# Second MLP product of an encoder layer: a fifth inner product in doubled form, its side work moved

## The chip, the core and the metric

The kernel runs on one core of a Trainium2 chip. The metric is the device time of one launch in microseconds (us), from the first instruction to the last. TensorE (PE in the profile) multiplies, with its weight loads listed as PEld; VectorE (DVE), ScalarE (ACT) and GpSimd (POOL) work element by element; SyncE (SP) issues nearly all transfers, which sixteen DMA engines carry out.

## The reference

One encoder layer on a sequence of 2048 tokens with 1024 channels, in fp32. Only its last lines matter here:

```python
x = x + gt1 * (mixed @ w_o[l])
h = rmsnorm(x, g_norm2[l]) * (1.0 + sc2) + sh2
x = x + gt2 * (jnp.square(jax.nn.relu(h @ w1[l])) @ w2[l])
```

The first MLP product multiplies 2048x1024 by `w1` (1024x4096), the second 2048x4096 by `w2` (4096x1024). What stands ahead of them (modulation, input projection, two kinds of attention) is not touched.

## The kernel before

Everything is held transposed: channels on the 128 partitions, 512 tokens (`TB`) to a tile. A number in fp32 is split into a rounded high part and the rest (`split`): ScalarE copies the high part, VectorE subtracts it from the number to get the low part. A product is then three matmuls, high by high, high by low, low by high (`mm3`, line 206). The pair of parts of one 128x512 tile is called an operand here. It lies in one of the 8 buffers of the pool `opp` (line 1297).

**Seven products instead of eight.** Both MLP products are written as 2x2 block products by Strassen's method in Winograd's form. The seven inner products are numbered `OUTER` = 1, 5, 6, 3, 7, 2, 4; each is the product of a sum of blocks of the weights and a sum of blocks of the activations.

**The order of the work.** A list `steps` is run from front to back. Ahead of each step operands of later steps are prepared as long as no more than 8 tiles are held (line 1949). Other work is hung on a step's number by `at(n, job)`. PE and SP run in the order in which the program issues; a scheduler sets the order of VectorE and ScalarE when the program is built, and it is fixed from then on. The second half of the kernel is this list:

- 8 `Mixed` steps: rest of the output projection.
- For `mb` = 1: 112 `First` steps (16 column pairs `j` by seven inner products): the first MLP product for half of the tokens. A step is 12 matmuls. Its results are relu'd, squared, and kept as block sums in `scr_hid` in HBM.
- `plain(1, i)` for `i` in `PLAIN` (line 1284): inner product `i` of the second MLP product for `mb` = 1, 16 `Second` steps of 12 matmuls each (4 output tiles by 3).
- For `mb` = 0: 112 `First` steps again.
- `plain(0, 1)`, `outer(7)`, `plain(0, 6)`, `outer(2)`, `plain(0, 5)`, `outer(3)`, `outer(4)` (line 1891 on).

**The doubled form.** `outer(i)` (line 1791) does inner product `i` of both halves `mb` at once by a second level of the same method: again seven products `pr`, each of 8 `Outer` steps with 6 matmuls, so 56 steps and 336 matmuls, where the plain form takes 192 for each `mb`. It needs more besides. An `Outer` step takes one operand `opr` of the activations, and every second step one operand `ol` of the weights: 84 operands. `half` loads activation sums into `halves`, and `half_sum` makes three more sums of them, for `pr` = 6, 7 and 4 (4 subtractions on VectorE each, 128x1024). `outer_sums` (line 1677) makes the weight sums of the second level beforehand, during the `First` steps of `mb` = 0, and stores them in `scr_t`. When a product ends, its PSUM result is added straight into tiles of the residual by `weigh` (lines 1627 and 1761): one tile for `i` = 2, 3 and 4, two for `i` = 7, at six of the products and for two banks each, so 12 or 24 instructions. The plan for `half` and `half_sum` is written down by step numbers (lines 1894 to 1902), the gap between the four of one kind being two steps.

**Plain products** instead collect 1, 6 and 5 in a shared sum `Second.whole["s", n]` in SBUF, and `update` (line 1634) loads residual tiles, adds that sum by `weigh`, and stores them: after product 6 four tiles, after product 5 twelve, for each `mb`.

**The second normalization** of `mb` = 0 (`norm2`) leaves its row factors in `rows`, in the two buffers of pool `rp`. `right_blocks` (line 1372) then makes the right-hand blocks of the first MLP product out of the residual for each of 4 values `k`: load, multiply by the factors, shift, and a chain of splits and subtractions (15 on VectorE per `k`). For `mb` = 0 this runs beside `plain(1, ...)`, ten steps to a `k`, in six pieces.

## Time and profile before

| | |
|---|---|
| median of three runs | 2552.38 us (2550.7 to 2552.95) |
| the profiled execution | 2549.72 us, span 2548.0 us |
| busy in the span | PE 99%, PEld 83%, DVE 79%, ACT 59%, POOL 29% |
| granted TensorE clock | 1.00 in every slice |
| transfers | 698.92 MB, mean 274 GB/s |
| second half of the kernel, from 1315.47 us | `First` of `mb` = 1 from 1359.0, plain products from 1668.4, `First` of `mb` = 0 from 1798.9, `plain(0, 1)` from 2103.57, `outer(7)` from 2149.37, `plain(0, 6)` from 2226.37, `outer(2)` from 2270.24, `plain(0, 5)` from 2346.40, `outer(3)` from 2389.92, `outer(4)` from 2466.08 |

In a line of the trace the names of tiles tell the stage: `opw` and `h` belong to `First`, `oph` and `opv` to the plain products, `opr`, `ol` and `r` to the doubled ones (`r<-r,r` is a `half_sum`), `txo` and `cxo` to `weigh` in a doubled product, `txu` and `xu` to `update`. Nearly all lines stand under L42, since a helper records the operations. A matmul's duration in the trace (389 ns) contains the pipeline; what it costs is the time from one start to the next. The same holds for VectorE, whose instructions begin a little before the one ahead of them has ended.

### The profile page before, as it was taken

The numbers are of one execution on the slowest core, as the hardware profiler recorded it, in microseconds if no ns is written. First come the engines' busy times: TensorE is split into PE (matmuls) and PEld (weight loads), VectorE is DVE, ScalarE is ACT, GpSimd is POOL, SyncE is SP. The second block draws the span as 40 slices with busy tenths as digits, with TensorE's granted clock in tenths as the row PEclk, the third lists the DMA queues.
The fourth block names the chain that finished last, engine by engine and source line by source line (L and its number), as shares of the span: only waits on it lengthen the run. The fifth ranks groups of instructions, "written<-read, shape, count | busy, mean of one in ns | idle before, by whom it ended". The sixth has DMA issues, their size and how long they took to land.

```text
span 2548.0 us, 39355 instructions
## 1 busy us (share of the span) xinstructions
PE 2520.9 (99%) x12436; PEld 2104.0 (83%) x12436; DVE 2010.0 (79%) x3509; ACT 1498.6 (59%) x2871; POOL 747.0 (29%) x1128
## 2 busy tenths in 40 slices
PE   9999999999999999999999999999999999999999
PEld 7888888888888888887988888888888887888887
DVE  7656767887789878998858777668988766988897
ACT  6333425668866677666755555566555555656565
POOL 4330154776776667776620000000000000000000
PEclk9999999999999999999999999999999999999999
DMA  9879979779987788866787888787899889777772
GB/s 359 327 295 365 348 269 295 216 243 291 284 237 235 239 251 269 268 211 196 230 301 253 301 284 281 257 312 260 279 323 303 264 274 394 273 285 271 281 266 83
DMA packets 293200, 698.92 MB, mean 274 GB/s; under 512 B 31360, under 2 KB 83584, under 8 KB 281856
## 3 DMA queue, kind: packets, MB, share of 16 engines
q1 hardware_dynamic: 291696, 691.69, 79.7%
q10 hardware_dynamic: 1296, 4.72, 0.5%
q8 instruction: 98, 1.61, 0.3%
q14 instruction: 110, 0.90, 0.1%
HBM read 477.66 MB, written 218.63 MB: 273 GB/s over the span
## 4 chain that ended last, share of the span: by engine, by line
PE 83%; DVE 6%; DMA 3%; ACT 3%; issue 2%; POOL 1%; SPq 0%; DVEq 0%; ACTq 0%; POOLq 0%
PE ps L42 27%; PE ps_s L42 14%; PE pt L42 11%; PE acc L42 6%; PE wt L42 6%; PE pf L42 4%; PE z L42 4%; PE po L42 4%; PE pq L42 3%; DVE p L42 2%; PE cz L42 2%; DMA hw<-in_w_dram 1%; PE ct L42 1%; DVE opr L42 1%; ACT z L42 1%
## 5 line engine op out<-in xcount | busy, mean ns | idle before, releaser
L42 PE MATMUL ps<-h,opw 128*128 128x512 f32 x1512 | 358.6, 389 | 0.0
L42 ACT CAST wth<-wt 128x512 fp32r<-128x512 f32 (+3 forms) x544 | 257.3, 484 | 166.0 <-PE wt L42 156.9
L42 POOL TENSOR_TENSOR b<-p 128x512 f32<-128x512 f32 (+1 forms) x320 | 292.5, 914 | 168.0 <-DVE p L42 95.0
L42 DVE TENSOR_TENSOR wtl<-wt,wth 128x512 fp32r<-128x512 f32 (+3 forms) x544 | 291.2, 547 | 57.6 <-ACT wth L42 55.8
L42 PEld LDWEIGHTS ps<-h,opw 128*128 128x128 f32 x1512 | 283.7, 188 | 58.8
L42 PE MATMUL pt<-w,ht 128*128 128x512 f32 x1248 | 288.2, 391 | 0.0
L42 PE MATMUL ps_s<-h,opw 128*128 128x512 f32 x1152 | 277.3, 389 | 0.4 <-ACT ps_s L42 0.4
L42 PEld LDWEIGHTS pt<-w,ht 128*128 128x128 f32 x1248 | 232.9, 188 | 47.7
L42 DVE TENSOR_TENSOR_SCAN p<-z,p,zero 128x512 f32<-128x512 f32 x192 | 245.8, 1281 | 25.7 <-ACT z L42 18.1
L42 PE MATMUL ps<-oph,opv 128*128 128x512 f32 x1152 | 263.2, 390 | 1.2 <-ACT opv L42 1.1
L42 PEld LDWEIGHTS ps<-oph,opv 128*128 128x128 f32 x1152 | 216.0, 188 | 47.8 <-ACT opv L42 1.9
L42 PEld LDWEIGHTS ps_s<-h,opw 128*128 128x128 f32 x1152 | 215.9, 188 | 46.0 <-ACT ps_s L42 0.8
L42 PE MATMUL acc<-wth,v 128*128 128x512 f32 (+3 forms) x544 | 220.6, 410 | 0.0
L42 ACT CAST opr<-r 128x512 fp32r<-128x512 f32 x224 | 139.7, 625 | 105.5 <-PE ps L42 50.6
L42 ACT ACTIVATE z<-z 128x512 f32<-128x512 f32 (+1 forms) x320 | 166.4, 520 | 55.3 <-PE z L42 48.9
L42 PE MATMUL z<-k,q 128*128 128x512 f32 (+3 forms) x640 | 185.7, 372 | 7.7 <-DVE p L42 7.0
L42 PE MATMUL acc<-wtl,v 128*128 128x512 f32 (+3 forms) x544 | 185.5, 347 | 0.0
L42 PE MATMUL ps<-opr,ol 128*128 128x512 f32 x768 | 176.4, 389 | 0.1
L42 PE MATMUL wt<-ident,b 128*128 128x128 f32 x1088 | 171.4, 273 | 0.9 <-DVE p L42 0.6
L42 DVE TENSOR_TENSOR opr<-r,opr 128x512 fp32r<-128x512 f32 x224 | 151.3, 689 | 25.9 <-ACT opr L42 23.3
L42 PEld LDWEIGHTS wt<-ident,b 128*128 128x128 f32 x1088 | 136.4, 141 | 41.4 <-DVE wtl L42 1.9
L42 PEld LDWEIGHTS ps<-opr,ol 128*128 128x128 f32 x768 | 144.0, 188 | 30.5 <-DVE ol L42 0.4
(214 smaller groups left out, 4846.9 us busy)
## 6 DMA issues: line engine op xcount, KB each, us to landing
q<-scr_q SPq DMA_DIRECT2D x128, 256.0 KB, 5.5
w<-in_w_dram SPq DMA_DIRECT2D x64, 512.0 KB, 5.5
r<-scr_hid SPq DMA_DIRECT2D x64, 512.0 KB, 8.0
k<-scr_k SPq DMA_DIRECT2D x240, 128.0 KB, 4.5
v<-scr_v SPq DMA_DIRECT2D x120, 256.0 KB, 4.2
wa<-in_w_ada_dram SPq DMA_DIRECT2D x48, 512.0 KB, 6.2
ow<-scr_wo SPq DMA_DIRECT2D x24, 1024.0 KB, 6.2
hw<-scr_hid SPq DMA_DIRECT2D x48, 512.0 KB, 6.4
```

The lines of the kernel that those rows point to most:

```text
L42: return lambda *x, **y: self.tc.keep_in_program_order(f(*x, **y))
```

## The change

Inner product 5 of the second MLP product moves from the plain to the doubled form. `PLAIN` becomes 1 and 6, `DOUBLE` 7, 5, 2, 3, 4, and the order behind the `First` steps of `mb` = 0 becomes `plain(0, 1)`, `outer(7)`, `plain(0, 6)`, `outer(5)`, `outer(2)`, `outer(3)`, `outer(4)`. With it:

- `outer(5)` adds into two residual tiles per bank (24 instructions). Its activation blocks need one more subtraction (`half_sum` for `pr` = 5, four of 128x1024), which runs in `outer(7)`.
- The weight sums are made for 7, 5, 3 and 4 in the `First` steps of `mb` = 0, seven steps earlier than before; those of product 2 are made in the second half of the `First` steps of `mb` = 1, by the new `narrow_sums` (32 subtractions of 128x256 instead of 16 of 128x512 elements).
- The twelve `update` tiles that followed product 5 move. Those of `mb` = 1 go into the first half of the `First` steps of `mb` = 0, four steps apart, in the two buffers of pool `rp` that held the norms; those of `mb` = 0 go into `outer(2)` (eight) and `outer(3)` (four).
- `right_blocks` for `mb` = 0 runs in ten pieces (the new `chain`), six steps to a `k`, since there are 32 plain steps of `mb` = 1 now instead of 48.
- The step numbers of `half` and `half_sum` change.

In numbers of built instructions: 48 matmuls fewer, 72 transfers more, and on VectorE 20 operand parts, 16 half sums, 24 `weigh` and 32 narrow sums more and 8 `column_sum` into the shared sum fewer.

```diff
@@ -1281,8 +1281,8 @@
     NP = DFF // P // 2
     HK = KT // 2
-    PLAIN = (1, 6, 5)
-    DOUBLE = (7, 2, 3, 4)
+    PLAIN = (1, 6)
+    DOUBLE = (7, 5, 2, 3, 4)
     OUTER = (1, 5, 6, 3, 7, 2, 4)
     OUTER_NAME = {1: "11", 2: "12", 4: "22"}
     HOME = {1: 1, 2: 1, 5: 5, 3: 5, 6: 6, 7: 6, 4: 6}
@@ -1429,7 +1429,16 @@
                 low(6, "22")
                 low(4, "21")
-            return load, scale, mixed, rest, multiply, shift, begin
+            def chain():
+                yield low(1, "11"), low(3, "22"), less("11", "12", "11")
+                yield high(5, "11"), low(2, "21"), less("12", "22", "12")
+                yield high(7, "12"), low(5, "11"), less("22", "22", "11")
+                yield high(6, "22"), low(7, "12"), less("21", "21", "22")
+                yield high(4, "21"), low(6, "22")
+                yield low(4, "21"), None
+
+            steps_of = chain()
+            return load, scale, mixed, rest, multiply, shift, begin, lambda: next(steps_of)
         class Step:
@@ -1621,8 +1630,6 @@
                     act.copy(d["s", n], ps)
                 if i == 6:
                     column_sum(dve, d["s", n], ps, d["s", n], ALU.add)
-                if i == 5:
-                    column_sum(dve, d["s", n], ps, d["s", n], ALU.add)
         def weigh(x, a, n):
             dve.scalar_tensor_tensor(x, a, mod[:, 5 * KT + n : 5 * KT + n + 1], x, op0=ALU.mult, op1=ALU.add)
@@ -1653,25 +1660,9 @@
             f = len(steps)
             steps.extend(Second(mb, i, j) for j in range(NP))
-            spread = lambda *ns: [f + n for n in ns]
             if i == 6:
+                spread = lambda *ns: [f + n for n in ns]
                 update(mb, 0, 1, spread(0, 1, 2, 8), spread(4, 5, 6, 12))
-            if i == 5:
-                update(mb, 1, 1, spread(1, 2, 3, 9), spread(6, 7, 8, 13))
-                wide = []
-
-                def slot(nm):
-                    if not wide:
-                        t = raw_pair([P, HK, TB], F32, nm)
-                        wide.extend(t[:, n, :] for n in range(HK))
-                    return wide.pop(0)
-
-                if mb:
-                    update(mb, 0, 0, spread(11, 11, 11, 11), spread(16, 16, 17, 17), slot)
-                    update(mb, 1, 0, spread(13, 13, 14, 14), spread(18, 18, 19, 19), kept)
-                else:
-                    update(mb, 0, 0, spread(11, 12, 13, 14), spread(16, 17, 18, 19))
-                    update(mb, 1, 0, spread(15, 16, 17, 21), spread(20, 21, 22, 25), None, True)
             return f
         def outer_sums(i, m, step):
@@ -1681,7 +1672,7 @@
             def load():
                 t.append(raw_pair([P, 2, 2, TB], F32, f"wt{i}_{m}"))
                 for a in range(2):
-                    if i in (3, 7):
+                    if i in (3, 7, 5):
                         sp.dma_start(t[0][:, a], scr_s[i - 1 if i < 7 else 0, HP // 2 * a + m])
                         continue
                     r, s = {2: (0, 1), 4: (1, 1)}[i]
@@ -1695,6 +1686,27 @@
                 later.add(2, lambda: sp.dma_start(scr_t[i, pr][:, 2 * m : 2 * m + 2, :], v[dst]))
             at(step - 6, load)
+            todo = ((5, "22", "21", "22", ALU.add), (7, "21", "11", "21", ALU.subtract))
+            todo += ((6, "11", "22", "11", ALU.subtract), (3, "12", "12", "11", ALU.subtract))
+            for n, x in enumerate(todo):
+                at(step + n, lambda x=x: sums(*x))
+
+        def narrow_sums(i, k, step):
+
+            t = []
+            r, s = {2: (0, 1), 4: (1, 1)}[i]
+
+            def load():
+                for a in range(2):
+                    t.append(temp(f"wn{i}_{k}_{a}"))
+                    sp.dma_start(t[a], w2[2 * (HP * a + k) + s][:, r * TB : (r + 1) * TB])
+
+            def sums(pr, dst, a, b, op):
+                v = {nm: t[h][:, c * CN : (c + 1) * CN] for nm, h, c in (("11", 0, 0), ("12", 1, 0), ("21", 0, 1), ("22", 1, 1))}
+                column_sum(dve, v[dst], v[a], v[b], op)
+                later.add(2, lambda: sp.dma_start(scr_t[i, pr][:, k, :], v[dst]))
+
+            at(step - 4, load)
             todo = ((5, "22", "21", "22", ALU.add), (7, "21", "11", "21", ALU.subtract))
             todo += ((6, "11", "22", "11", ALU.subtract), (3, "12", "12", "11", ALU.subtract))
             for n, x in enumerate(todo):
@@ -1717,7 +1729,7 @@
                     sp.dma_start(t, scr_t[i, pr])
                     return
                 a, h = {1: (0, 0), 2: (1, 0), 4: (1, 1)}[pr]
-                if i in (3, 7):
+                if i in (3, 7, 5):
                     for m in range(HP // 2):
                         src = scr_s[i - 1 if i < 7 else 0, HP // 2 * a + m]
                         sp.dma_start(t[:, 2 * m : 2 * m + 2], src[:, :, h * CN : (h + 1) * CN])
@@ -1764,14 +1776,14 @@
                             later.add(2, lambda dst=dst, x=x: sp.dma_start(dst, x))
             def load_x(self, b):
-                home = kept if self.i == 7 and b in ("22", "11") else temp
+                home = kept if self.i in (5, 7) and b in ("22", "11") else temp
                 for n in range(2):
                     Outer.outs[b, n] = []
-                    for r, odd in {2: ((0, 1),), 3: ((0, 0),), 4: ((1, 1),), 7: ((1, 1), (1, 0))}[self.i]:
+                    for r, odd in {2: ((0, 1),), 3: ((0, 0),), 4: ((1, 1),), 7: ((1, 1), (1, 0)), 5: ((0, 0), (1, 0))}[self.i]:
                         mb, row = 2 - int(b[1]), HK * r + 2 * (int(b[0]) - 1) + n
                         x = home(f"xo{self.i}_{b}_{n}{odd}")
                         sp.dma_start(x, scr_x[2 * mb + odd, row])
-                        Outer.outs[b, n].append((x, mb, row, odd, self.i != 7 or (mb and not odd)))
+                        Outer.outs[b, n].append((x, mb, row, odd, self.i in (2, 3, 4) or (self.i == 5 and mb and r)))
         halves = {}
@@ -1783,6 +1795,9 @@
         def half_sum(i, pr, g):
+            if pr == 5:
+                column_sum(dve, halves[5, g], halves[5, g], halves[1, g], ALU.subtract)
+                return
             x, y = {6: (3, 5), 7: (6, 1), 4: (2, 6)}[pr]
             t = hop[g].tile([P, 2, TB], F32, tag=f"h{pr}_{g}", name=f"r{i}_{pr}_{g}")
             column_sum(dve, t, halves[x, g], halves[y, g], ALU.subtract)
@@ -1858,8 +1873,10 @@
                 f = steps[begin + 7 * j]
                 if mb:
                     second_sums(j, begin + 7 * j + 2)
+                    if j >= HP:
+                        narrow_sums(2, j - HP, begin + 71 + 5 * (j - HP))
                 else:
-                    outer_sums(DOUBLE[j // 4], j % 4, begin + 7 * j + 5)
+                    outer_sums((7, 5, 3, 4)[j // 4], j % 4, begin + 7 * j - 2)
                     if j < HP:
                         for i, n in ((3, 2), (2, 5), (7, 2), (4, 5)):
                             at(begin + 7 * j + n, lambda i=i, f=f: f.other(i))
@@ -1872,14 +1889,19 @@
                 norm2(1, begin + 18)
                 norm2(0, begin + 48)
                 for k in range(HK):
-                    begins = end + 1 + 10 * k
-                    pieces = right_blocks(0, k, temp)
-                    for n, m in ((0, 0), (4, 4), (5, 5), (6, 6), (7, 2), (9, 3)):
+                    begins = end + 6 * k
+                    pieces = right_blocks(0, k, kept if k % 2 else temp)
+                    for n, m in ((0, 0), (4, 4), (5, 5), (6, 6), (7, 7), (8, 7), (9, 7), (10, 7), (11, 7), (12, 7)):
                         at(begins + n, pieces[m])
                 for i in PLAIN:
                     plain(1, i)
                 for n in range(end, len(steps), 2):
                     at(n - 7 - max(0, end + 4 - n) // 2, steps[n].load)
+                rest = len(steps)
+                lent = lambda nm: rp.tile([P, TB], F32, tag="r", name=nm)
+                for n, (r, odd) in enumerate(((0, 0), (1, 1), (1, 0))):
+                    at_row = rest + 3 + 16 * n
+                    update(1, r, odd, range(at_row, at_row + 16, 4), range(at_row + 4, at_row + 20, 4), lent)
             else:
                 at(begin - 8, steps[begin].load)
                 at(begin - 6, steps[begin].fetch)
@@ -1889,17 +1911,25 @@
                 at(f + m - (leads.pop(0) if leads else 7), steps[f + m].load)
         f = plain(0, 1)
-        plain_loads(f, [9])
+        plain_loads(f, [9, 9, 9, 8, 8, 8])
         e = len(steps)
-        plan = {"load": {1: (f - 5, 1), 5: (f - 1, 1), 3: (f + 4, 2), 2: (f + 18, 2)}}
-        plan["sum"] = {6: (f + 9, 2), 7: (f + 13, 2), 4: (f + 44, 2)}
-        for i, p in ((7, 6), (2, 5), (3, None), (4, None)):
+        plan = {"load": {1: (f - 3, 1), 5: (f + 2, 2), 3: (f + 10, 2), 2: (f + 18, 2)}}
+        plan["sum"] = {6: (f + 16, 2), 7: (f + 21, 2), 4: (f + 44, 2)}
+        for i in DOUBLE:
             f = outer(i, plan)
             e = len(steps)
-            if p:
-                plain_loads(plain(0, p), [12, 11, 11, 11, 9, 8])
-            plan = {"load": {1: (f + 6, 2), 5: (f + 17, 2), 3: (f + 30, 2), 2: (f + 46, 2)}}
-            plan["sum"] = {6: (e + 1 if i == 7 else f + 38, 2), 7: (e + 4, 2), 4: (e + 8, 2)}
+            if i == 7:
+                plain_loads(plain(0, 6), [12, 11, 11, 11, 9, 8])
+            spread = lambda *ns: [f + n for n in ns]
+            if i == 2:
+                update(0, 0, 0, spread(18, 22, 26, 30), spread(24, 28, 32, 36))
+                update(0, 1, 1, spread(36, 40, 44, 48), spread(42, 46, 50, 54))
+            if i == 3:
+                update(0, 1, 0, spread(12, 16, 20, 24), spread(17, 21, 25, 29), None, True)
+            plan = {"load": {1: (f + 22, 2), 5: (f + 17, 2), 3: (f + 30, 2), 2: (f + 46, 2)}}
+            plan["sum"] = {6: ({7: e + 1, 5: e - 4}.get(i, f + 38), 2), 7: (e + (8 if i == 7 else 16), 2), 4: (e + (16 if i == 7 else 26), 2)}
+            if i == 7:
+                plan["sum"][5] = (f + 31, 2)
         blocks = [right_blocks(1, k, kept if k else temp) for k in range(HK)]
```

## Prediction, made before the changed kernel ran

> **What bounds the kernel now.** I read the busy times first, then the chain of work that ended last, then the busy times stage by stage, and then single instructions inside the doubled products.
>
> ```profile
> PE 2520.9 (99%) x12436; PEld 2104.0 (83%) x12436; DVE 2010.0 (79%) x3509; ACT 1498.6 (59%) x2871; POOL 747.0 (29%) x1128
> PE 83%; DVE 6%; DMA 3%; ACT 3%; issue 2%; POOL 1%; SPq 0%; DVEq 0%; ACTq 0%; POOLq 0%
> ```
>
> TensorE is busy 99% and carries 83% of the chain: the time is its number of matmuls times its pace, plus what it waits. The stages, in order: the first row is `First` of `mb` = 1, the next three the plain products 1, 6, 5 of `mb` = 1, then `First` of `mb` = 0, `plain(0, 1)`, `outer(7)`, `plain(0, 6)`, `outer(2)`, `plain(0, 5)`, `outer(3)`, `outer(4)`. The first number behind the window is its length, then busy times.
>
> ```profile
> 1359.00:1668.37 309.37, 309.00 (x1378) 255.66 (x1376) 224.28 (x358) 173.32 (x306) 3.62 (x10) 1.00 0.79 277
> 1668.37:1711.89 43.52, 43.52 (x194) 36.05 (x192) 32.21 (x53) 27.50 (x49) 0.00 (x0) 1.00 0.80 290
> 1711.89:1755.41 43.52, 43.52 (x194) 36.05 (x192) 36.28 (x60) 29.28 (x52) 0.00 (x0) 1.00 0.69 255
> 1755.41:1798.93 43.52, 43.52 (x194) 36.05 (x192) 40.60 (x67) 26.51 (x47) 0.00 (x0) 1.00 0.83 290
> 1798.93:2103.57 304.64, 304.64 (x1346) 252.34 (x1344) 233.12 (x370) 161.65 (x285) 0.00 (x0) 1.00 0.88 289
> 2103.57:2149.37 45.80, 44.66 (x193) 35.82 (x192) 26.82 (x40) 21.10 (x38) 0.00 (x0) 1.00 1.04 402
> 2149.37:2226.37 77.00, 76.90 (x338) 62.83 (x336) 74.86 (x115) 51.03 (x88) 0.00 (x0) 1.00 0.80 291
> 2226.37:2270.24 43.87, 43.83 (x193) 35.96 (x192) 39.71 (x55) 18.57 (x32) 0.00 (x0) 1.00 0.74 287
> 2270.24:2346.40 76.16, 76.16 (x337) 63.06 (x336) 66.19 (x102) 50.57 (x86) 0.00 (x0) 1.00 0.73 261
> 2346.40:2389.92 43.52, 43.52 (x193) 36.04 (x192) 34.16 (x49) 18.31 (x32) 0.00 (x0) 1.00 0.79 287
> 2389.92:2466.08 76.16, 76.16 (x337) 63.06 (x336) 70.55 (x110) 50.58 (x86) 0.00 (x0) 1.00 0.80 282
> 2466.08:2543.80 77.72, 77.37 (x337) 62.58 (x335) 66.71 (x100) 46.99 (x80) 0.00 (x0) 1.00 0.37 127
> ```
>
> A doubled product's 336 matmuls take 76.16 us (0.2267 us each, 1.36 us a step of six), a plain product's 192 take 43.52. VectorE's share in a doubled product is 86 to 97%, against 74% in the first plain one. So VectorE is the second bound there, and the change puts four such products in a row without the plain product that stood between 2 and 3. Here is where TensorE already loses time in them, and in `plain(0, 1)`:
>
> ```profile
> 2131.64 6.01 PE L42 MATMUL ps<-oph,opv 128*128 128x512 f32 x24 [0.71 <-ACT opv L42]
> 2182.01 11.04 PE L42 MATMUL ps<-opr,ol 128*128 128x512 f32 x48
> 2192.89 11.44 PE L42 MATMUL ps_s<-opr,ol 128*128 128x512 f32 x48
> 2204.17 11.48 PE L42 MATMUL ps<-opr,ol 128*128 128x512 f32 x48
> 2215.49 11.04 PE L42 MATMUL ps_s<-opr,ol 128*128 128x512 f32 x48
> ...
> 2487.86 6.30 PE L42 MATMUL ps_s<-opr,ol 128*128 128x512 f32 x25
> 2494.41 5.90 PE L42 MATMUL ps_s<-opr,ol 128*128 128x512 f32 x23 [0.25 <-DVE opr L42]
> 2500.14 11.04 PE L42 MATMUL ps<-opr,ol 128*128 128x512 f32 x48
> ```
>
> Eight steps should go by in 10.88 us. In `outer(7)` steps 32 to 40 took 11.28 (2192.89 to 2204.17) and steps 40 to 48 took 11.32: 0.84 lost. In `outer(4)` steps 16 to 24 took 12.28 (2487.86 to 2500.14): 1.40 lost. `plain(0, 1)` lost 45.80 - 43.52 = 2.28, on transfers (below).
>
> VectorE's prices are the times from one start to the next:
>
> ```profile
> 2185.35 0.69 DVE L42 TENSOR_TENSOR ol<-l,ol 128x512 fp32r<-128x512 f32 x1
> 2185.96 1.29 DVE L42 TENSOR_TENSOR opr<-r,opr 128x512 fp32r<-128x512 f32 x2
> 2187.16 0.69 DVE L42 TENSOR_TENSOR ol<-l,ol 128x512 fp32r<-128x512 f32 x1
> ...
> 2189.57 1.22 DVE L42 TENSOR_TENSOR r<-r,r 128x1024 f32<-128x1024 f32 x1
> 2190.70 1.29 DVE L42 TENSOR_TENSOR opr<-r,opr 128x512 fp32r<-128x512 f32 x2
> ...
> 2194.25 2.72 DVE L42 SCALAR_TENSOR_TENSOR txo<-ps,mod,txo 128x512 f32<-128x512 f32 x4
> 2196.88 0.69 DVE L42 TENSOR_TENSOR opr<-r,opr 128x512 fp32r<-128x512 f32 x1
> ```
>
> A low part of an operand costs 0.602 us (1.81 for three), a half sum 1.13, a `weigh` 0.657 (2.63 for four); an `update` I take like a `weigh`.
>
> **The change part by part.**
>
> *Matmuls.* Out go 2 x 192 = 384, in come 336: 48 x 0.2267 = 10.9 us less. TensorE is the bound, so all of it counts.
>
> *VectorE in the doubled products.* I count the instructions between the first operand part of one stage and that of the next, in the built order. Before: `outer(7)` 84 operand parts, 10 half sums, 20 weighs = 75.0 us; `outer(2)` 65.2; `outer(3)` 71.1; `outer(4)` 68.8. Against 76.16 all fit. After:
> - `outer(7)`: 84 parts (50.6), 16 half sums (18.1; its own twelve now all lie inside it, and the four for `pr` = 5 are new), 20 weighs (13.1): 81.8, which is 5.6 too many.
> - `plain(0, 6)`: 32.4 of 43.52, room for 11.
> - `outer(5)`: 71.8.
> - `outer(2)`: 84 parts, 16 half sums, 14 weighs, 7 updates: 82.5, which is 6.3 too many.
> - `outer(3)`: 75.3, and `outer(4)` 68.8 as before.
>
> A mean is not enough: VectorE works its list in the built order, and only as far ahead as eight operand tiles allow. So I keep an account of its lag. A step gives it 1.36 us, and 1.5 operand parts take 0.90, so it gains 0.46 a step until it is level; every sum sets it back 1.13, a pair of weighs 1.31, four 2.63. What lag does TensorE bear? Before, in `outer(7)`, sums at steps 28 to 34 and four weighs at 32 and 40 make a lag of 4.4, then 4.3, and 0.84 was lost; in `outer(4)`, eight sums at steps 4 to 14 and two weighs make 5.8, and 1.40 was lost. Both say that about 4 us are borne (3.5 to 4.4) and the rest is lost.
>
> After, `outer(7)`: eight sums at steps 0 to 11 and four weighs at 8 make 6.6, so 2.6 lost; level by 24; eight sums at 28 to 37 and four weighs at 24 and 32 make 8.4, so 4.4 lost; four weighs at 40 add 1.3. Sum 8.3. `outer(5)`: its weighs at the end meet the first sums of the next product at a lag of 5.0: 1.0. `outer(2)`: pairs of sums and updates from step 16 to 54 make 8.3, so 4.5 lost. `outer(3)`: sums at 16 to 44 make 7.4, so 3.4 lost. `outer(4)`: 0.5. Together 17.7 if 4 us are borne, 20 at 3.5, 14.4 at 4.5; the lower end is the overload of the means less 4 us carried over at each of the two places, 4. I take 16, near the account since it is gauged in the same stages. Less the 2.2 lost there before: 13.8 more.
>
> One page speaks harder against this change. The Trainium skill, "VectorE: DVE Perf Modes", section "The DRAIN you can't avoid", says that the next operation does not start until the pipe has emptied, so that whole durations would add up (0.69, 1.22 and 0.68): `outer(7)` would then need 91 us and `outer(2)` 92, the five products would lose some 45, and the time would be near 2588. The rows differ: starts lie 0.60 apart at a duration of 0.69, and `outer(3)` of before, which would need 80 by that rule, lost nothing. The measurement decides.
>
> *Weight sums and loads of `plain(0, 1)`.* It gets its data with less crowding: its half sums move into `outer(7)`, the weight sums end seven steps earlier. Of the 2.28 lost I let 2.0 go; bounds 0 and 2.28. ScalarE, whose busy time in the doubled stages is at most 51 of 76, stays cover.
>
> *Plain products of `mb` = 1.* The four chains of `right_blocks` now lie in 32 steps instead of 48. In the built order VectorE has 38.7 us of work in `plain(1, 1)` and 47.8 in `plain(1, 6)`, of 43.52 each: 4.3 too many in the second, before which there is room. Bounds 0 and 4.3; I take 1.5, since a plain step uses two tiles in 2.72 us, and lag is borne for longer.
>
> *Narrow sums.* In the second half of `First` of `mb` = 1 come 16 loads, 32 stores and 32 subtractions; VectorE's mean there is 72% (224.28 of 309.37), so it is cover. What can be late is one sum that waits for its load, with the reads of PSUM queued behind it. The nearest row of a `First` stage:
>
> ```profile
> DVE ts L42 <- DMA scr_hid<-to: 11.9, 7, 2.2
> ```
>
> The longest was 2.2: bounds 0 and two of those, 4.4; I take 1.5.
>
> *Updates and transfers in `First` of `mb` = 0.* Twelve `update` tiles with 24 transfers come into its first half, where the DMA engines are at their highest of any stage with full pace:
>
> ```profile
> 1875.00:1913.00 38.00, 38.00 (x170) 31.46 (x169) 31.39 (x51) 20.33 (x36) 0.00 (x0) 1.00 0.98 321
> 2126.00:2149.00 23.00, 21.86 (x93) 16.93 (x92) 13.89 (x20) 11.03 (x21) 0.00 (x0) 1.00 1.05 405
> ```
>
> The last number is GB/s, the one ahead of it the engines' busy share. 24 x 0.262 MB over 152 us are 41 GB/s more on 321; at the highest share that any row has (1.05, where TensorE lost time) this mix would carry 321 x 1.05 / 0.98 = 344. So up to 5% of 152 us, 8, could be late (a bound, since some of these transfers lay there before); 0 if it fits. The two buffers of `rp` make it worse: each is loaded again one step after its store, and behind that load SP's whole queue waits. I take 3.
>
> *Sum:* -10.9 + 13.8 - 2.0 + 1.5 + 1.5 + 3 = +6.9 us on the profiled 2549.72. That run stands 2.7 below the median of 2552.38; on the median I forecast 2559.3.
>
> **The rivals.**
>
> *Faster.* VectorE's lag costs TensorE little: the four operand tiles ahead bear 7 or 8 us rather than 4, so that only the overload of the means counts. Then 4 are lost in the doubled products instead of 16, and with nothing lost in the `First` stages the sum is -10.9 + 1.8 - 2.3 + 1 = -10, or 2542. For it: `outer(3)` of before, at 93% busy, lost nothing. Against it: both places where before lost time fit 4 us. It decides from a borne lag of about 6 us, where the sum crosses zero.
>
> *Transfers fall behind* in the first half of `First` of `mb` = 0: the 8 above, 4.4 in `First` of `mb` = 1, 3 in the plain products, the rest as forecast: -10.9 + 13.8 - 2 + 15.4 = +16, or 2569. For it: share 0.98 with 8% more to carry. Against it: most of that work waits there with a long lead.
>
> *The clock falls.* The granted clock is 1.00 in all rows, through a gap of 0.71 us too. A group of 48 matmuls at half the pace would cost another 10.9, and one in each of `outer(7)`, `outer(2)` and `outer(3)` would make 2592. The lost time comes in pieces no longer than a burst of weighs, so I give it little. The Trainium skill, "TensorE: Matmul & The Clock Gate", section "What's actually happening", has the clock fall to half after an idle window of some 3.4 us; no stretch of before is that idle, so no run here shows it.
>
> **How the numbers follow.** Forecast 0.62, faster rival 0.14, transfers 0.20, clock 0.04. A measurement here tells 0.2% (5.1 us) from no change, so slower begins at 2557.5. Of the forecast, whose own range is 2554 to 2567 (the borne lag from 5 down to 3.5), 0.44 lies above that and 0.18 within; of the faster rival 0.11 lies below 2547.3; of the transfers 0.20 and of the clock 0.04 above. So faster 0.11, same 0.21, slower 0.68. The range, with a tenth left out on each side: 2550 to 2572.
>
> **What would show it.** `outer(7)` about 84 us long and `outer(2)` about 81, with VectorE over 95% busy and TensorE waiting there for VectorE's `opr`; `outer(5)` near 77; `plain(0, 1)` near 43.7; `First` of `mb` = 0 at 305 to 308. I would be wrong if those two products stayed near 77, or if TensorE's waits named transfers instead.

## The result, and the profile after

The change makes the kernel 0.6% slower: 2566.96 us (median of four runs, 2565.59 to 2571.0) against 2551.98 us for the kernel before on the same chip (2550.7 to 2552.95). The ratio is 1.0062, with a 95% interval of 1.0044 to 1.0079: small, but clear of the noise. The forecast was 2559.3 with a range of 2550 to 2572. The profiled execution took 2567.03 us with a span of 2565.3, which is 17.3 more than the span of before.

The page of after, busy times and the chain of work that ended last:

```profile
PE 2523.2 (98%) x12388; PEld 2094.1 (82%) x12388; DVE 2054.8 (80%) x3593; ACT 1509.6 (59%) x2893; POOL 747.5 (29%) x1128
PE 71%; DVE 14%; DMA 7%; ACT 3%; issue 3%; POOL 1%; SPq 0%; DVEq 0%; ACTq 0%; POOLq 0%
```

TensorE has 48 instructions fewer, as announced. Its share of the chain fell from 83 to 71%; VectorE's rose from 6 to 14% and that of the transfers from 3 to 7%. Both are to be looked for in the stages. Busy times by stage in after: `First` of `mb` = 1, both plain products of `mb` = 1 together, `First` of `mb` = 0, `plain(0, 1)`, `outer(7)`, then behind `plain(0, 6)` `outer(5)`, `outer(2)`, `outer(3)`, `outer(4)`. The columns are those of the same view in the prediction.

```profile
1358.90:1668.55 309.65, 309.00 (x1377) 255.66 (x1376) 234.17 (x389) 172.86 (x306) 3.62 (x10) 1.00 0.85 299
1668.55:1757.33 88.78, 88.22 (x385) 71.94 (x384) 79.29 (x130) 64.27 (x113) 0.00 (x0) 1.00 0.77 285
1757.33:2074.83 317.50, 307.15 (x1345) 251.59 (x1344) 239.73 (x383) 161.96 (x288) 0.00 (x0) 1.00 0.88 298
2074.83:2118.35 43.52, 43.52 (x193) 36.05 (x192) 23.04 (x36) 21.18 (x38) 0.00 (x0) 1.00 0.89 348
2118.35:2201.87 83.52, 80.37 (x337) 62.22 (x336) 82.00 (x120) 50.87 (x88) 0.00 (x0) 1.00 0.75 282
...
2245.73:2321.89 76.16, 76.16 (x337) 63.06 (x336) 72.37 (x113) 50.46 (x86) 0.00 (x0) 1.00 0.74 270
2321.89:2403.71 81.82, 79.34 (x337) 62.26 (x336) 80.64 (x119) 50.41 (x86) 0.00 (x0) 1.00 0.78 268
2403.71:2483.82 80.11, 79.00 (x337) 62.31 (x336) 76.66 (x115) 50.00 (x86) 0.00 (x0) 1.00 0.90 307
2483.82:2560.90 77.08, 76.77 (x337) 62.72 (x335) 66.84 (x101) 46.93 (x80) 0.00 (x0) 1.00 0.39 132
```

Compared with the rows of before, stage by stage:

| stage | before | after | loss or gain |
|---|---|---|---|
| 48 matmuls fewer | | | -10.9 |
| the doubled products, over 76.16 each | 0.84 + 0 + 0 + 1.56 = 2.4 | 7.36 + 0 + 5.66 + 3.95 + 0.92 = 17.9 | +15.5 |
| `First` of `mb` = 0 | 304.64 | 317.50 | +12.9 |
| `plain(0, 1)` | 45.80 | 43.52 | -2.3 |
| plain products of `mb` = 1 | 43.52 each | 88.78 for two | +1.7 |
| `First` of `mb` = 1 | 309.37 | 309.65 | +0.3 |
| `plain(0, 6)`, and ahead of and behind these stages | | | +0.1 |
| sum | | | +17.3 |

So there are two large losses of nearly the same size: one in three doubled products, which was expected, and one in `First` of `mb` = 0, which was expected to be 3. The first of them in TensorE's timeline of after, from the start of `outer(7)` to its end:

```profile
2118.35 22.23 PE L42 MATMUL ps<-opr,ol 128*128 128x512 f32 x96
2140.43 12.06 PE L42 MATMUL ps_s<-opr,ol 128*128 128x512 f32 x48
2152.32 11.04 PE L42 MATMUL ps<-opr,ol 128*128 128x512 f32 x48
2163.20 5.83 PE L42 MATMUL ps_s<-opr,ol 128*128 128x512 f32 x25
2169.73 2.03 PE L42 MATMUL ps_s<-opr,ol 128*128 128x512 f32 x6 [0.70 <-DVE opr L42]
2172.07 3.77 PE L42 MATMUL ps_s<-opr,ol 128*128 128x512 f32 x12 [0.31 <-DVE opr L42]
2176.15 1.44 PE L42 MATMUL ps_s<-opr,ol 128*128 128x512 f32 x5 [0.31 <-DVE opr L42]
2177.42 6.80 PE L42 MATMUL ps<-opr,ol 128*128 128x512 f32 x25
2185.27 5.88 PE L42 MATMUL ps<-opr,ol 128*128 128x512 f32 x23 [1.04 <-DVE opr L42]
2190.99 11.04 PE L42 MATMUL ps_s<-opr,ol 128*128 128x512 f32 x48
```

From start to start, where eight steps should take 10.88: steps 0 to 16 took 22.08 (0.32 lost), 16 to 24 took 11.89 (1.01), 32 to 40 took 14.22 (3.34), 40 to 48 took 13.57 (2.69). TensorE waits for `opr`, which VectorE brings late. VectorE's timeline of after at that place:

```profile
2164.62 0.68 DVE L42 TENSOR_TENSOR opr<-r,opr 128x512 fp32r<-128x512 f32 x1
2165.22 1.21 DVE L42 TENSOR_TENSOR r<-r,r 128x1024 f32<-128x1024 f32 x1
2166.36 2.72 DVE L42 SCALAR_TENSOR_TENSOR txo<-ps,mod,txo 128x512 f32<-128x512 f32 x4
2169.00 0.68 DVE L42 TENSOR_TENSOR opr<-r,opr 128x512 fp32r<-128x512 f32 x1
```

It works without a gap. Between one `opr` (2164.62) and the next (2169.00) lie a half sum and four weighs, 4.38 us in which TensorE could have taken three steps.

The second loss: TensorE's waits in `First` of `mb` = 0 of after (us in total, times, longest). The same view of before lists no wait at all.

```profile
PE ps_s L42 <- DVE cp L42: 8.1, 6, 1.7
PE ps_s L42 <- ACT cp L42: 2.2, 2, 1.6
```

`cp` is the read of a PSUM bank that TensorE needs again; VectorE and ScalarE read it too late. What VectorE waited for in the first half of the stage (157 us), in after:

```profile
DVE ts L42 <- DMA scr_hid<-to: 23.5, 6, 5.2
```

In before the same row (in the prediction) had 11.9 in total and 2.2 at the longest. `ts` is a temporary tile that is free again when the store of the `to` that lay in it has landed. One of these waits in VectorE's timeline of after, and then the bank that came late in TensorE's:

```profile
1834.75 0.68 DVE L42 TENSOR_TENSOR wt<-wt 128x512 f32<-128x512 f32 x1
1840.65 0.69 DVE L42 TENSOR_TENSOR ts<-w 128x512 f32<-128x512 f32 x1 [5.22 <-DMA scr_hid<-to]
```

```profile
1849.01 3.03 PE L42 MATMUL ps_s<-h,opw 128*128 128x512 f32 x12 [1.57 <-ACT cp L42]
...
1856.34 3.06 PE L42 MATMUL ps_s<-h,opw 128*128 128x512 f32 x12 [1.58 <-DVE cp L42]
```

And what SP's queue waited for in that half, where all these stores are issued, in after:

```profile
SPq L42 <- DMA scr_x<-xu: 24.1, 10, 4.3
```

In before the row of the same name stands at 0.7:

```profile
SPq L42 <- DMA scr_x<-xu: 0.7, 2, 0.4
```

So ten times the queue stood until the store of an updated tile `xu` had landed, because the next thing in it was a load into that tile's buffer. Everything behind, the stores of `to` among it, was issued later. These views do not show that the one wait caused the other; that is the reading from which the experiments start.

### The profile page after: what moved, and what is told of

Read it like the earlier page. It is cut to its first block, busy times and chain, and to the rows that moved or that the text cites. A ratio compares the mean times of both kernels' runs of the same rounds, so it can differ in the third digit from the quotient of the medians.

```text
span 2565.3 us, 39482 instructions
## 1 busy us (share of the span) xinstructions
PE 2523.2 (98%) x12388; PEld 2094.1 (82%) x12388; DVE 2054.8 (80%) x3593; ACT 1509.6 (59%) x2893; POOL 747.5 (29%) x1128
## 4 chain that ended last, share of the span: by engine, by line
PE 71%; DVE 14%; DMA 7%; ACT 3%; issue 3%; POOL 1%; SPq 0%; DVEq 0%; ACTq 0%; POOLq 0%
PE ps L42 19%; PE pt L42 11%; PE ps_s L42 10%; PE acc L42 6%; PE wt L42 6%; PE pf L42 4%; PE z L42 4%; PE po L42 4%; DVE opr L42 3%; PE pq L42 3%; DVE r L42 2%; DVE p L42 2%; DMA scr_t<-wt 1%; PE cz L42 1%; DMA scr_hid<-to 1%
## 5 line engine op out<-in xcount | busy, mean ns | idle before, releaser
L42 ACT CAST opr<-r 128x512 fp32r<-128x512 f32 x280 | 174.2, 623 | 146.0 <-PE ps L42 69.7
L42 PE MATMUL ps<-opr,ol 128*128 128x512 f32 x960 | 223.6, 391 | 2.3 <-DVE opr L42 1.9
L42 PEld LDWEIGHTS ps<-opr,ol 128*128 128x128 f32 x960 | 179.2, 188 | 44.2 <-DVE opr L42 5.3
L42 DVE TENSOR_TENSOR opr<-r,opr 128x512 fp32r<-128x512 f32 x280 | 185.8, 686 | 18.3 <-ACT opr L42 17.0
L42 PE MATMUL ps_s<-opr,ol 128*128 128x512 f32 x720 | 172.9, 394 | 4.7 <-DVE opr L42 3.9
L42 PE MATMUL ps<-oph,opv 128*128 128x512 f32 x768 | 176.0, 390 | 0.6 <-DVE oph L42 0.2
L42 PEld LDWEIGHTS ps<-oph,opv 128*128 128x128 f32 x768 | 143.9, 188 | 32.2 <-DVE oph L42 1.2
```

Source lines behind the costliest of these rows:

```text
L42: return lambda *x, **y: self.tc.keep_in_program_order(f(*x, **y))
```

## The experiments

Each stands beside runs of the kernel before on the same chip. The theory had two parts. In the doubled products, VectorE's lag is what TensorE loses. In `First` of `mb` = 0, the two buffers of `rp` block SP's queue (theory A); its rivals are the bytes themselves and the twelve additions on VectorE. "Lost" is a stage's length over 304.64 (`First` of `mb` = 0) or 76.16 (a doubled product), read from the one profile of each kernel. Such a length varies by itself: where the code of `First` of `mb` = 0 is that of after, it took 317.50 (after), 317.27 (without the sum for product 5) and 321.20 us (half sums on GpSimd). Differences of up to 4 us in that stage therefore say little. The runs that leave something out, that with earlier stores and that with seven tiles were taken once each.

**The half sums on GpSimd.** VectorE is to be freed in the doubled products.

```diff
         def half_sum(i, pr, g):
             if pr == 5:
-                column_sum(dve, halves[5, g], halves[5, g], halves[1, g], ALU.subtract)
+                column_sum(pool, halves[5, g], halves[5, g], halves[1, g], ALU.subtract)
...
-            column_sum(dve, t, halves[x, g], halves[y, g], ALU.subtract)
+            column_sum(pool, t, halves[x, g], halves[y, g], ALU.subtract)
```

> All half sums of the doubled products are done by GpSimd instead of VectorE; nothing else is changed. Theory (VectorE's backlog in the doubled products costs the 17.9 us that TensorE loses there after the change): outer(7), outer(2), outer(3) and outer(4) go by in 76 to 77 us each, the time falls by 15 to 18 us against the changed kernel, to 2549 to 2552, level with the kernel before. Rival 1 (these products wait for transfers, VectorE merely looks busy): no change, 2567. Rival 2 (GpSimd is too slow for 128x1024, or slows VectorE down): the products stay at 80 us or more and the waits name r or a sum.

Measured: 2643.47 us against 2550.68, ratio 1.0352 (1.0333 to 1.0371). `outer(7)` took 111.4 us. VectorE's groups of this kernel from 2118 us on, shapes kept apart (busy, then mean ns of one, then idle before):

```profile
L42 DVE TENSOR_TENSOR opr<-r,opr 128x512 fp32r<-128x512 f32 x280 | 254.0, 923 | 33.3 <-ACT opr L42 31.3
L42 DVE SCALAR_TENSOR_TENSOR txo<-ps,mod,txo 128x512 f32<-128x512 f32 x26 | 18.1, 742 | 0.0
```

The group of operand parts in after:

```profile
L42 DVE TENSOR_TENSOR opr<-r,opr 128x512 fp32r<-128x512 f32 x280 | 185.8, 686 | 18.3 <-ACT opr L42 17.0
```

An operand part, whose two inputs lie in SBUF, went from 686 to 923 ns in the mean; a `weigh` (`txo`), which has one input in PSUM, took 742 (744 in after). An `update` (`txu`), the same operation with both inputs in SBUF, went from 745 to 1012. The timelines of the same kernel show the cause, VectorE first and then GpSimd:

```profile
2230.14 2.85 DVE L42 TENSOR_TENSOR opr<-r,opr 128x512 fp32r<-128x512 f32 x1
2232.92 2.86 DVE L42 TENSOR_TENSOR oph<-hw,oph 128x512 fp32r<-128x512 f32 x1
2235.70 0.68 DVE L42 TENSOR_TENSOR opv<-hw,opv 128x512 fp32r<-128x512 f32 x1
```

```profile
2221.32 13.90 POOL L42 TENSOR_TENSOR r<-r,r 128x1024 f32<-128x1024 f32 x5
2236.55 2.64 POOL L42 TENSOR_TENSOR r<-r,r 128x1024 f32<-128x1024 f32 x1 [1.33 <-DMA r<-scr_hid]
```

While GpSimd sums without a gap (to 2235.2), each operand part takes 2.85 us; in its gap one takes 0.68. Five sums take 13.90 us, 2.78 each, and VectorE's instructions start 2.78 apart: one of each goes by in turn. The longer operand parts alone cost VectorE 280 x 0.24 = 66 us for those of the activations and 140 x 0.28 = 39 us for those of the weights (685 ns in after, 962 here), more than the 64 x 1.13 = 72 us that the sums took there. This is rival 2, and the run doesn't test the account, since it doesn't free VectorE. The Trainium skill, "SBUF — State Buffer", section "Who interferes with whom", says that a VectorE instruction with two inputs in SBUF contends with a GpSimd instruction that reads SBUF, and that the pair of ports which they share is locked by one at a time. The rows agree, the untouched `txo` too.

**The updates of `mb` = 1 nine steps apart instead of four.** The same transfers and additions in the same two buffers, but over the whole stage, so that a store has time to land before its buffer is loaded again.

```diff
                 for n, (r, odd) in enumerate(((0, 0), (1, 1), (1, 0))):
-                    at_row = rest + 3 + 16 * n
-                    update(1, r, odd, range(at_row, at_row + 16, 4), range(at_row + 4, at_row + 20, 4), lent)
+                    at_row = rest + 3 + 36 * n
+                    update(1, r, odd, range(at_row, at_row + 36, 9), range(at_row + 4, at_row + 40, 9), lent)
```

> The twelve updates of mb = 1 lie nine steps apart over all of the First steps of mb = 0, instead of four steps apart in their first half. Theory (the updates crowd SP's queue and the transfers there, a load into a reused buffer waits for the store out of it, and with it the stores that free VectorE's tiles): First of mb = 0 goes from 317.5 us to 305 to 307, the time falls by 10 to 12, to 2555 to 2557. Rival 1 (VectorE's 12 more instructions are the cause, wherever they lie): as many are issued, so 312 or more is left. Rival 2 (the weight sums that moved seven steps ahead are the cause): no change, 317.

Measured: 2554.57 us against 2550.68, ratio 1.0015 (1.0005 to 1.0024). `First` of `mb` = 0 in this kernel:

```profile
1755.53:2061.12 305.59, 305.43 (x1346) 251.99 (x1344) 239.71 (x383) 161.81 (x288) 0.00 (x0) 1.00 0.91 307
```

0.95 is lost instead of 12.86, as theory A forecast, with the same 383 instructions on VectorE, and the doubled products lose what they lost in after (17.9). The stage's mean rate is even higher (307 against 298 GB/s).

**Both together.**

> The half sums on GpSimd and the updates nine steps apart together. If both theories hold, the gains add: 15 to 18 and 10 to 12, less nothing, so 2538 to 2542, which is some 11 to 13 us less than the kernel before (48 matmuls are 10.9 us, and the 4.5 us that it loses in plain(0, 1) and in its own doubled products go too, against 2 in the plain products of mb = 1). If the two losses were one and the same (a backlog carried along), the sum would fall short, at 2548 or more.

Measured: 2626.74 us, ratio 1.0294 (1.0279 to 1.031), about 17 less than with the sums on GpSimd alone, and far from the 2538 to 2542 that were forecast, since the sums on GpSimd do harm. `First` of `mb` = 0 took 304.68 us here, against 321.20 with the sums on GpSimd alone: the spread takes that stage's loss away a second time.

**Without the updates of `mb` = 1.**

```diff
-                    update(1, r, odd, range(at_row, at_row + 16, 4), range(at_row + 4, at_row + 20, 4), lent)
+                    pass
```

> The twelve updates of mb = 1 behind the plain products are left out, with their loads, additions and stores (three quarters of the residual rows of that half lack the sum of products 1 and 6). Theory (the updates are the cause of the loss in First of mb = 0): that stage goes by in 304.6 to 306 us, the rest as in the changed kernel, so 2554 to 2556. Rival (the earlier weight sums, or the transfers without the updates): 312 to 317 us.

Measured: 2554.04 us; `First` of `mb` = 0 took 304.71, so 0.07 is lost, and the doubled products lost 17.9. The whole loss of `First` of `mb` = 0 hangs on these twelve tiles, and none of that of the doubled products.

**The updates without their stores.** Loads and additions stay.

```diff
-                later.add(3, lambda: sp.dma_start(dst, x))
+                if stored:
+                    later.add(3, lambda: sp.dma_start(dst, x))
...
-                    update(1, r, odd, range(at_row, at_row + 16, 4), range(at_row + 4, at_row + 20, 4), lent)
+                    update(1, r, odd, range(at_row, at_row + 16, 4), range(at_row + 4, at_row + 20, 4), lent, stored=False)
```

> In the changed kernel the twelve updates of mb = 1 are loaded and added at their crowded places, but not stored (so those residual rows lack the sum). Theory A (the store that has to land before the next load into its buffer blocks SP's queue, and with it the stores that free VectorE's tiles): First of mb = 0 goes from 317.5 to 305 to 308 us. Theory B (VectorE's twelve additions in a stage that is 80% full): 315 or more. Theory C (the bytes themselves): half of them are gone, so the stage lies half way, near 311.

Measured: 2553.1 us, stage 304.69: 0.05 lost. Loads and additions alone cost nothing here. This leaves the bytes of the stores or the wait for them.

**The stores two steps earlier.** The bytes stay the same and only the time between a store and the load behind it grows: `later` holds a store back for three steps, here for one.

```diff
-                later.add(3, lambda: sp.dma_start(dst, x))
+                later.add(ticks, lambda: sp.dma_start(dst, x))
...
-                    update(1, r, odd, range(at_row, at_row + 16, 4), range(at_row + 4, at_row + 20, 4), lent)
+                    update(1, r, odd, range(at_row, at_row + 16, 4), range(at_row + 4, at_row + 20, 4), lent, ticks=1)
```

> In the changed kernel each of the twelve updates of mb = 1 is stored right after its addition instead of two steps later. Same loads, additions, stores, bytes and buffers; only the store into HBM has 5.4 us more until the next load into its buffer, which before had about one step. Theory A (SP's queue blocked by the landing of that store): First of mb = 0 loses at most half of its 12.9 us, so it takes 304.6 to 311 us. Theory C (the bytes): no change, 315 to 318 us.

Measured: 2557.75 us against 2549.35, one run each. The stage took 307.29, so 2.65 is lost. SP's and VectorE's waits in its first half, in this kernel:

```profile
SPq L42 <- DMA scr_x<-xu: 3.7, 5, 1.6
```

```profile
DVE ts L42 <- DMA scr_hid<-to: 14.0, 6, 3.2
```

The queue stands 3.7 us instead of 24.1, VectorE's longest wait falls from 5.2 to 3.2, and four fifths of the loss are gone, with all the bytes still there. That is theory A against the bytes. VectorE's wait is not the price by itself: without the updates it still waited 16.9 us in that half, 3.3 at the longest, and only 0.07 was lost.

**The updates without their additions.** All 24 transfers stay, the twelve `weigh` go.

```diff
-                weigh(x, Second.whole["s", n], row)
+                if weighed:
+                    weigh(x, Second.whole["s", n], row)
...
-                    update(1, r, odd, range(at_row, at_row + 16, 4), range(at_row + 4, at_row + 20, 4), lent)
+                    update(1, r, odd, range(at_row, at_row + 16, 4), range(at_row + 4, at_row + 20, 4), lent, weighed=False)
```

> In the changed kernel the twelve updates of mb = 1 are loaded and stored at their places, but nothing is added (those rows lack the sum), so VectorE has 7.9 us less to do there. Theory A (transfers and SP's queue): the loss in First of mb = 0 stays mostly, 313 to 318 us. Theory B (VectorE's additions): it goes, 305 to 308 us.

Measured: 2560.68 us, stage 311.87: 7.23 lost of 12.86, which lies between the two forecasts. SP's queue stands as long as in after (23.3 us, 11 times). Some 1.6 of the 7.23 us are a slower clock behind one long wait (last section). So the transfers and the blocked queue alone cost 5.6 to 7.2 us here, about half. The other half comes only with the additions, 12 x 0.66 = 7.9 us of VectorE, though these cost nothing where the queue does not stand, as the run without stores shows. That VectorE then lacks this time for making up its lag is likely; no run shows it by itself.

**Without the sum for product 5 in `outer(7)`.** This tests the account of VectorE's lag: four half sums at steps 31 to 37 less.

```diff
             if pr == 5:
-                column_sum(dve, halves[5, g], halves[5, g], halves[1, g], ALU.subtract)
                 return
```

> In the changed kernel the four half sums for pr = 5 in outer(7) are left out, so outer(5) multiplies wrong blocks. By the account of the lag outer(7) then loses 2.6 and 1.2 instead of 8.3, that is 4.5 less than with them: it goes from 83.5 us to 79 and the time to 2562.5; all later products keep their length. Rival (VectorE's instructions at another price than their own 1.13 us each, or the loss coming from the transfers of these halves): 82 us or more, since loads and everything else stay.

Measured: 2563.91 us. `outer(7)` in this kernel:

```profile
2119.88:2198.84 78.96, 78.33 (x337) 62.45 (x336) 77.45 (x116) 50.91 (x88) 0.00 (x0) 1.00 0.79 296
```

It loses 2.80 instead of 7.36. Four sums are 4 x 1.13 = 4.5 us of VectorE, and TensorE gets back 4.56: beyond what the tiles ahead bear, a microsecond of VectorE was one of TensorE here. The loads of these halves are still there, so the rival by which the transfers cost the time falls.

**Seven operand tiles ahead instead of eight.**

```diff
-            while nxt is not None and ready - used + nxt.tiles <= 8 and nxt.ready():
+            while nxt is not None and ready - used + nxt.tiles <= 7 and nxt.ready():
```

> In the changed kernel operands are prepared up to seven tiles ahead instead of eight. One tile is 0.91 us of TensorE's time (4 matmuls), so the lag that is borne falls from 4 to 3.1 us. Theory (the account): the five doubled products lose 22 to 23 us instead of 17.9, each but the first part of outer(5) a little more: some 5 us slower in these stages. Rival (the products are bound by VectorE's mean alone, so how far ahead it may work does not matter): within 1 us of 17.9.

Measured: 2566.49 us. The five doubled products lose 8.36, 0, 6.65, 4.48 and 1.48, together 21.0 instead of 17.9. That is 3.1 more, where the account had 4 to 5 and the rival at most 1. So the borne lag does hang on the tiles held ahead, by somewhat less than forecast: a tile is worth 0.5 to 1.0 us in each product where something was lost. In this run the plain products of `mb` = 1 lost 3.7 instead of 1.7, `First` of `mb` = 0 lost 8.9 instead of 12.9, a difference of the size by which that stage varies by itself, and the total stayed.

**Other places for sums and updates.** Beside the spread of nine steps, the sums and updates of the doubled products are moved to where VectorE has room: the four sums for `pr` = 5 from `outer(7)` into `plain(0, 6)`, the sums for `pr` = 6 from the end of a product to the start of the next, sums mostly three steps apart instead of two, and four update tiles each in `outer(2)`, `outer(3)` and `outer(4)` instead of eight, four and none.

```diff
             if i == 2:
-                update(0, 0, 0, spread(18, 22, 26, 30), spread(24, 28, 32, 36))
-                update(0, 1, 1, spread(36, 40, 44, 48), spread(42, 46, 50, 54))
+                update(0, 0, 0, spread(26, 32, 38, 44), spread(32, 38, 44, 50))
             if i == 3:
-                update(0, 1, 0, spread(12, 16, 20, 24), spread(17, 21, 25, 29), None, True)
+                update(0, 1, 1, spread(4, 10, 16, 22), spread(10, 16, 24, 30))
+            if i == 4:
+                update(0, 1, 0, spread(30, 34, 38, 42), spread(36, 40, 44, 48), None, True)
...
-            plan["sum"] = {6: ({7: e + 1, 5: e - 4}.get(i, f + 38), 2), 7: (e + (8 if i == 7 else 16), 2), 4: (e + (16 if i == 7 else 26), 2)}
+            plan["sum"] = {6: (e + (9 if i == 7 else 0), 3 if i != 7 else 2), 7: (e + (22 if i == 7 else 14), 3), 4: (e + (36 if i == 7 else 28), 3)}
             if i == 7:
-                plan["sum"][5] = (f + 31, 2)
+                plan["sum"][5] = (e + 1, 2)
```

> From the kernel with the updates nine steps apart. All half sums and updates are done on VectorE as before, as many of them, but at other steps: the four sums for pr = 5 go from outer(7) into plain(0, 6), the sums for pr = 6 of the next product from the end of one product to the start of the next, the four of one kind lie three steps apart instead of two, and four updates each go to outer(2), outer(3) and outer(4) instead of eight and four to outer(2) and outer(3). Theory (a backlog over about 4 us is what costs TensorE time, so the place of the work counts and not its amount): the five doubled products lose some 5 us instead of 17.9, the time falls from 2554.6 to 2541 to 2545, below the kernel before. Rival (VectorE's total is what counts, which nothing here changes): 2553 to 2556.

Measured: 2542.88 us (six runs, 2540.63 to 2543.29) against 2550.57, ratio 0.9968 (0.9956 to 0.9981). By 0.3%, this version is faster than the kernel before, and by 0.9% faster than after. Its five doubled products:

```profile
2106.01:2184.99 78.98, 78.35 (x338) 62.44 (x336) 77.46 (x116) 50.90 (x88) 0.00 (x0) 1.00 0.79 297
2228.85:2307.04 78.19, 77.34 (x337) 62.91 (x336) 76.30 (x117) 50.45 (x86) 0.00 (x0) 1.00 0.71 260
2307.04:2383.51 76.47, 76.47 (x338) 62.98 (x336) 76.26 (x115) 50.45 (x86) 0.00 (x0) 1.00 0.82 294
2383.51:2460.69 77.18, 76.77 (x337) 62.98 (x336) 75.29 (x113) 50.45 (x86) 0.00 (x0) 1.00 0.83 298
2460.69:2536.85 76.16, 76.16 (x337) 62.88 (x335) 72.17 (x108) 46.91 (x80) 0.00 (x0) 1.00 0.45 153
```

They lose 2.82, 2.03, 0.31, 1.02 and 0, together 6.2 instead of 17.9. VectorE's busy times now lie between 72.2 and 77.5, where they were between 66.8 and 82.0. The sum of VectorE's work is the same (3593 instructions in both), so its total is not what counted. The 48 matmuls less are worth 10.9 us, of which 7.7 remain on the median; where the side work lay had taken back more than all of it. The sums and the updates moved together here, so this run does not tell what each was worth.

Not tried: a third buffer for `rp`, and the weight sums at their old place, seven steps later.

## Why the prediction came out as it did

The direction and the range were right; the size was 7.7 us short. One term alone was 9.9 short, and 2.7 came back by chance (below). That 2566.96 still lies within the forecast's own range of 2554 to 2567 is luck: that range stood for a borne lag between 5 and 3.5 us, and the missing time lay in another stage. Of its signs, those on the doubled products and on `plain(0, 1)` came as described, with VectorE over 98% busy in `outer(7)` and `outer(2)`; that on `First` of `mb` = 0, 305 to 308 us, did not.

- *Matmuls*: -10.9 as stated, 12388 instead of 12436.
- *VectorE in the doubled products*: right in mechanism and nearly in size. The account gave 17.7, of which 16 were taken; 17.9 was lost. By product: 8.3 forecast and 7.4 measured in `outer(7)`, 1.0 and 0 in `outer(5)`, 4.5 and 5.7 in `outer(2)`, 3.4 and 4.0 in `outer(3)`, 0.5 and 0.9 in `outer(4)`. Each is off by up to 1.2, and the errors cancel in the sum. In `outer(7)` the early sums cost 1.3 instead of 2.6 and the later ones 6.0 instead of 5.7. The four microseconds that the tiles bear, read from two places in the trace of before, held that far; the runs without the sum for product 5 and with one tile less show that it is this lag that TensorE pays for. The faster rival, by which 7 or 8 us would be borne, fell. It speaks of four operand tiles ahead, but eight are held; at four matmuls each they are 7.25 us, of which about 4 were borne.
- *Whole durations added up*, the harder price, would have lost some 45 in the five products; 17.9 was lost, so the distance from start to start is the price here. The Trainium skill, "VectorE: DVE Perf Modes", section "The DRAIN you can't avoid", adds that a next operation that is not held starts earlier, which the prediction leaves out; the starts 0.60 us apart at a duration of 0.69 agree with that.
- *`plain(0, 1)`*: -2.3 measured, -2.0 taken; no run tests which of the two reasons given did it. *Plain products of `mb` = 1*: +1.7 measured, +1.5 taken.
- *Narrow sums*: +0.3 measured, 1.5 taken. That VectorE was cover there fits.
- *Updates and transfers in `First` of `mb` = 0*: this step failed. 3 was taken with an upper bound of 8; 12.9 was lost. The bound was worked out from bytes per second against the highest share in any row, and bytes were not the price: the same bytes cost 0.9 when spread over the stage and 2.7 when only stored earlier. The step named the right place, the two buffers of `rp` behind which SP's whole queue waits, and then gave it no price of its own. The queue's wait could have been bounded from the transfers of before in that stage (KB each, then median us from issue to landing):

```profile
scr_x<-xu SPq DMA_DIRECT2D x4, 256.0 KB, 7.0
```

With one step of 2.72 us between store and load, each of the ten loads into a used buffer could hold the queue for some 4.3 us (an estimate); in after the longest wait was 4.3, and the ten made 24.1. How much of that reaches TensorE no row of before tells. The rival *Transfers fall behind* gave 2569 for the sum of such losses and was near in time, but by 8 there, 4.4 in `First` of `mb` = 1 and 3 in the plain products, which were 12.9, 0.3 and 1.7; and the 8% more to carry that it names are 13% by its own numbers, 41 on 321.

- *The clock*: 1.00 in every stage of after, through waits of up to 1.7 us. In three other runs it did fall in `First` of `mb` = 0, behind waits of 2.05 to 2.58 us (last section).

On the spans the sum was +6.9 and came out as +17.3: 9.9 too little in `First` of `mb` = 0, 1.7 in the doubled products, 1.2 too much for the narrow sums, and some tenths. The forecast then added 2.7 for the distance of the profiled run of before to its median; the profiled run of after lies at its median, which takes 2.7 off the error. That is chance, not a part of the working.

## What to carry to other kernels

A load into a buffer whose store is still under way holds everything behind it in an in-order queue: price it by the waits that it can set off (here 24.1 us in ten) and by who needs the transfers behind it, not by bytes, and leave as many steps between store and load as a landing takes (here 7 us, nearly three steps). Where an engine works ahead of TensorE by a few tiles, keep an account of its lag step by step, gauged in places of the trace where TensorE already loses time; a mean share says little (`outer(5)` lost nothing with VectorE 95% busy, `outer(3)` 3.95 us at 96%), and moving the same work to where there is room won back 11.7 of 17.9 us here. Before work goes to GpSimd, look whether VectorE reads two SBUF tiles at the same time.

## What the runs showed of the hardware that was not expected

While GpSimd summed out of SBUF, a VectorE instruction with two inputs in SBUF took 2.85 us instead of 0.68, one of each in turn, 2.78 us apart; a `weigh` with one input in PSUM took 742 ns as ever.

The clock fell in the kernel with the half sums on GpSimd, at several places. In the stretch of 10 us shown here it is 0.65 (the number ahead of the last two), in the one before it 1.00:

```profile
2220.00:2230.00 10.00, 5.21 (x12) 2.97 (x12) 10.00 (x4) 1.95 (x4) 10.00 (x5) 0.65 0.70 279
```

TensorE's timeline there:

```profile
2221.97 1.65 PE L42 MATMUL ps_s<-opr,ol 128*128 128x512 f32 x5 [2.27 <-DVE ol L42]
2224.74 3.56 PE L42 MATMUL ps_s<-opr,ol 128*128 128x512 f32 x7 [1.13 <-DVE opr L42]
```

Seven matmuls take 3.56 us, about half a microsecond each, behind waits of 2.27 and 1.13 us that lie close together. But two waits are not needed. In `First` of `mb` = 0 of the run without additions, the clock fell behind a single wait; a stretch of 10 us, and TensorE's timeline in it:

```profile
1847.00:1857.00 10.00, 7.42 (x26) 5.71 (x25) 6.51 (x12) 4.77 (x9) 0.00 (x0) 0.83 1.05 383
```

```profile
1852.13 4.61 PE L42 MATMUL ps_s<-h,opw 128*128 128x512 f32 x12 [2.58 <-DVE cp L42]
```

The same stage in the run without the sum for product 5, where the stretch around this line has 0.83 too:

```profile
1938.63 4.61 PE L42 MATMUL ps_s<-h,opw 128*128 128x512 f32 x12 [2.05 <-DVE cp L42]
```

And twice with the half sums on GpSimd, where the clock is 1.00 around the first line and 0.83 around the second:

```profile
1920.52 3.06 PE L42 MATMUL ps_s<-h,opw 128*128 128x512 f32 x12 [2.35 <-DVE cp L42]
...
1942.21 4.60 PE L42 MATMUL ps_s<-h,opw 128*128 128x512 f32 x12 [2.31 <-DVE cp L42]
```

So twelve matmuls took 4.6 us instead of 3.06 behind single waits of 2.05, 2.31 and 2.58 us, but not behind one of 2.35; what decides between them is not shown. In after, where the longest wait is 1.7 us, the clock stayed at 1.00. The Trainium skill, "TensorE: Matmul & The Clock Gate", section "What's actually happening", has the clock fall to half after an idle window of about 3.4 us. The rows show it fall behind waits shorter than that.
